# Shift and scale of three column blocks by GpSimd products and ScalarE sums

## The chip, the cores and the metric

The kernel runs on one core of a Trainium2 chip. It is written with the Bass and Tile layers, so the engines of the core (TensorE or PE, VectorE or DVE, ScalarE or ACT, GpSimd or POOL, and SyncE or SP, which here only issues transfers) each run their own list of instructions in order and wait for one another by semaphores. Data lie in the core's SBUF (128 partitions), TensorE writes into PSUM, and transfers between HBM and SBUF are done by 16 DMA engines that take their work from queues.

The metric is the device time of one execution in microseconds; given is the median over several runs. Lower is better.

## The reference

One layer of an adaLN-modulated mixer, D = 2048, 512 latent tokens and 256 context tokens, all in float32. Cut to what matters here:

```python
silu_c = jax.nn.silu(c); silu_cc = jax.nn.silu(c_ctx)
shift, scale, gate       = split(silu_c  @ w_ada + b_ada, 3)     # w_ada: 2048 x 6144
shift_c, scale_c, gate_c = split(silu_cc @ w_ada + b_ada, 3)
h  = rmsnorm(x)   * (1 + scale)   + shift        # 512 x 2048, latent tokens
hc = rmsnorm(ctx) * (1 + scale_c) + shift_c      # 256 x 2048, context tokens
p  = h @ w_in                                    # q, k, v, gates, Fourier input ...
kc, vc = (hc @ w_in)[k and v columns]
y  = merge(attention(q, [k, kc], [v, vc]), fourier_mix(u), gates) @ w_out
out = rmsnorm(x + gate * y)
```

Shift and scale are two vectors of 2048 values for the latent tokens, and two for the context. Each is a product of a row with a 2048 x 2048 matrix. `gate` is needed only at the end, and the context's pair not before the context's rows are made.

## The kernel before, in words

**Precision.** Products of tokens with weights are split: every weight piece `wr` (128x1024, 512 KB) becomes a high part `whi` by a ScalarE copy (L181) and a low part `wlo` by a VectorE subtraction (L182), and TensorE does three products with them (`mm3`, L339 to L341). Most of the kernel is "groups", in which w_in's products are formed by a fast algorithm on such pieces, about 77 us each, and after them the attention with the projections.

**The start stage** (to about 150 us) makes shift and scale, the normalised rows `h` and, as soon as a row block of `h` is there, a first set of products with it (the "start pieces", `w_start`). The 2048 columns are cut into 16 blocks of 128, `kb` = 0 to 15. For block `kb`:

- `wada_load(kb)` brings its weights, two tiles `wa` of 1 MB (pool "wada", four of them, so two blocks at a time), laid out with the input rows on the partitions;
- `modulate(kb)` calls `matvec` (L567) twice: 2 x 16 TensorE instructions of 8 for each half and each k (32 columns of `c2` as the stationary side, of which the first two are silu(c) and silu(c_ctx), 256 weight columns as the moving one: 128 for shift, 128 for scale). In the trace a line of it is `pd<-wa,c`. Both vectors, c and c_ctx, thus cost one pass;
- `taken(kb)` (L583) copies the sums from PSUM to SBUF by ScalarE (tile `ado`); `turned(kb)` (L588) turns them onto the partitions by two TensorE transposes; `factors(kb)` adds the partial sums on VectorE and makes `gain` and `shift`;
- `make_h(kb)` makes the row: VectorE multiplies by gain and by the root (L631), ScalarE adds the shift and rounds to the high part (L632), VectorE makes the low part (L634).

From block 6 on the blocks go in pairs (the loop `for kb in range(4, KK - 4, 2)`, with `k = kb + 2`, so pairs 6/7, 8/9, 10/11, 12/13; 14 and 15 come singly). In a pass of this loop TensorE first works off pieces of the start products with `some(n)`, in between two pieces are split (`split_next`), then come the products of the two blocks, one step of pieces, the four transposes and the two rows.

**What sets the order.** In the start stage PE, ACT and DVE run in the order in which the program writes their instructions (`manual_schedule`). SyncE's loads are chained in the order of `ask` and `load_start`, since each is issued after the last one; a weight tile of the pool must be free before its load is issued. GpSimd's list is the scheduler's; in the start it holds the transfers of the rotary tables: two loads into `S3` and `Z5`, and `rot_d`, which writes the finished tables to DRAM (L767).

**Groups.** Group after group, each in the steps P1, Q5, P2, Q6, P7, Q3, Q4 with four pieces each. Besides, the vector `gate` is made there on VectorE, without TensorE: `use_gate` (L1369) multiplies a piece of `w_gate` (128 output columns on the partitions, 1024 inputs along the row) by silu(c), spread over all partitions in `crow`, and sums along the row. 32 such products are spread by the table GATE_AT over groups 1, 2, 3 and 5, and the rest into the attention. The row is loaded as `c` by GpSimd's queue (`load_row`, first half at the end of group 0, second half at group KV + 1) and made into 2 silu(c) by a ScalarE tanh and one VectorE product (`silu_of_row`); one of the two calls stands in the attention, at step 3.

## Time and profile before

| | |
|---|---|
| median of 3 runs | 1286.51 us (1286.42 to 1286.75) |
| the profiled execution | 1286.97 us |
| its span, first to last instruction | 1285.2 us |
| mean granted clock of TensorE | 0.999 |
| instructions of TensorE, VectorE, ScalarE, GpSimd | 6562, 1305, 1077, 226 |
| VectorE's product and sum for `gate`, each (L1369) | 1217 ns, 32 of them |

The page of the profile gives for each engine the time that it was busy and its share of the span; then the chain of waits, followed back from the last instruction; and groups of equal instructions with their mean time. The timeline lists instructions of one engine in time order: start, length, engine, line, operation, output and inputs, shape, count, and in square brackets how long the engine waited before and for what. The windows give each engine's busy time in stretches of the span. Times are microseconds from the start of the span.

### The profile page before, as it was taken

How to read it: one execution, taken by the hardware profiler on the slowest of the kernel's cores; microseconds unless marked ns; L12 is line 12 of the kernel's file. 1: busy time of each engine (PE TensorE's matmuls, PEld its weight loads, DVE VectorE, ACT ScalarE, POOL GpSimd, SP SyncE). 2: the span in 40 equal slices, each digit the busy share in tenths (PEclk: the TensorE clock that was granted, in tenths of full speed). 3: DMA queues.
4: the chain of work that ended last, by engine and by line, in shares of the span. 5: the costliest groups of instructions: out<-in, count | busy, mean ns of one | idle time of the engine just before them, and what ended most of it. 6: DMA issues, size and time to landing. Idle time of an engine off the chain costs nothing.

```text
span 1285.2 us, 17638 instructions
## 1 busy us (share of the span) xinstructions
PE 1269.6 (99%) x6562; PEld 1045.2 (81%) x6562; DVE 991.0 (77%) x1305; ACT 683.2 (53%) x1077; POOL 173.2 (13%) x226
## 2 busy tenths in 40 slices
PE   8999999999999999999999999999999999999997
PEld 5677888888888888888888888888888888888886
DVE  5767899889778787748687756778898777787677
ACT  5322765555466564543355445766667646465544
POOL 0000121111102011012021011011100221211310
PEclk9999999999999999999999999999999999999999
DMA  9998798888898998887879897578852989998986
GB/s 378 412 368 344 242 204 254 229 240 239 234 315 209 320 271 254 291 197 188 282 204 288 254 259 234 180 234 250 265 178 67 260 241 258 245 207 222 227 207 179
DMA packets 104343, 319.07 MB, mean 248 GB/s; under 512 B 9889, under 2 KB 32801, under 8 KB 100289
## 3 DMA queue, kind: packets, MB, share of 16 engines
q1 hardware_dynamic: 54336, 195.24, 41.8%
q0 software_dynamic: 27600, 100.29, 37.0%
q10 hardware_dynamic: 22320, 22.42, 5.1%
q8 instruction: 51, 0.84, 0.3%
q14 instruction: 36, 0.29, 0.1%
HBM read 283.30 MB, written 34.61 MB: 247 GB/s over the span
## 4 chain that ended last, share of the span: by engine, by line
PE 82%; DVE 3%; DMA 2%; ACT 2%; issue 1%; SPq 0%; ACTq 0%
PE banks L339 10%; PE banks L340 10%; PE banks L341 10%; PE x L341 9%; PE x L339 9%; PE x L340 9%; PE y L341 8%; PE y L340 8%; PE y L339 8%; PE banks L1551 2%; DMA wr<-in_w_pab 1%; DVE wlo L182 1%; DMA s<-yb_d 1%; PE banks L1665 1%; DVE s L182 0%
## 5 line engine op out<-in xcount | busy, mean ns | idle before, releaser
L181 ACT ACTIVATE whi<-R 128x1024 fp32r<-128x1024 f32 x138 | 145.1, 1058 | 143.7 <-PE banks L341 47.5
L182 DVE TENSOR_TENSOR wlo<-R,whi 128x1024 fp32r<-128x1024 f32 x138 | 167.7, 1221 | 61.2 <-ACT whi L181 60.9
L182 DVE TENSOR_TENSOR wlo<-wr,whi 128x1024 fp32r<-128x1024 f32 (+1 forms) x122 | 147.3, 1213 | 62.7 <-ACT whi L181 62.5
L181 ACT ACTIVATE whi<-wr 128x1024 fp32r<-128x1024 f32 (+1 forms) x122 | 127.4, 1050 | 123.4 <-PE y L341 33.0
L339 PE MATMUL banks<-whi,s 128*128 128x512 f32 (+1 forms) x400 | 157.8, 394 | 0.9 <-ACT ev L1160 0.7
L340 PE MATMUL banks<-wlo,s 128*128 128x512 f32 (+1 forms) x400 | 155.9, 390 | 0.0
L341 PE MATMUL banks<-whi,s 128*128 128x512 f32 (+1 forms) x400 | 155.8, 389 | 0.0
L339 PE MATMUL x<-whi,s 128*128 128x512 f32 x352 | 137.1, 390 | 0.0
L341 PE MATMUL x<-whi,s 128*128 128x512 f32 x352 | 137.0, 389 | 0.0
L340 PE MATMUL x<-wlo,s 128*128 128x512 f32 x352 | 136.9, 389 | 0.0
L292 POOL DMA_DIRECT2D R<-in_w_g x68 | 59.5, 874 | 484.7 <-DVE wlo L182 290.2
L340 PE MATMUL y<-wlo,s 128*128 128x512 f32 x316 | 123.0, 389 | 0.1
L339 PE MATMUL y<-whi,s 128*128 128x512 f32 x316 | 122.9, 389 | 0.0
L341 PE MATMUL y<-whi,s 128*128 128x512 f32 x316 | 122.8, 389 | 0.0
L181 ACT ACTIVATE s<-wr 128x512 fp32r<-128x512 f32 (+2 forms) x93 | 60.8, 677 | 66.0 <-DMA wr<-cf_d 24.4
L182 DVE TENSOR_TENSOR s<-wr,s 128x512 fp32r<-128x512 f32 (+2 forms) x93 | 66.7, 749 | 31.8 <-ACT s L181 30.9
L339 PEld LDWEIGHTS banks<-whi,s 128*128 128x128 f32 x400 | 75.2, 188 | 16.6 <-ACT ev L1160 1.1
L341 PEld LDWEIGHTS banks<-whi,s 128*128 128x128 f32 x400 | 75.2, 188 | 15.3
L340 PEld LDWEIGHTS banks<-wlo,s 128*128 128x128 f32 x400 | 75.2, 188 | 13.9 <-DVE wlo L182 0.2
L340 PEld LDWEIGHTS x<-wlo,s 128*128 128x128 f32 x352 | 66.1, 188 | 13.8
L341 PEld LDWEIGHTS x<-whi,s 128*128 128x128 f32 x352 | 66.1, 188 | 13.7
L339 PEld LDWEIGHTS x<-whi,s 128*128 128x128 f32 x352 | 66.1, 188 | 13.6
(333 smaller groups left out, 2794.0 us busy)
## 6 DMA issues: line engine op xcount, KB each, us to landing
wr<-in_w_g SPq DMA_DIRECT2D x124, 512.0 KB, 5.6
R<-in_w_g POOLq DMA_DIRECT2D x68, 512.0 KB, 7.4
wa<-in_w_ss SPq DMA_DIRECT2D x31, 1024.0 KB, 9.5
R<-in_w_g SPq DMA_DIRECT2D x32, 512.0 KB, 5.8
wr<-in_w_gate SPq DMA_DIRECT2D x32, 512.0 KB, 5.1
wr<-in_w_o SPq DMA_DIRECT2D x24, 512.0 KB, 7.1
R<-in_w_o POOLq DMA_DIRECT2D x24, 512.0 KB, 8.9
wr<-in_w_pab SPq DMA_DIRECT2D x20, 512.0 KB, 6.1
```

What stands on the lines that cost most here:

```text
L181: first = nc.scalar.activation(hi, src, ACT.Copy)
L182: return first, nc.vector.tensor_tensor(lo, src, hi.bitcast(F32), op=ALU.subtract)
L292: chained[:] = [nc.gpsimd.dma_start(chain[e.pc], e.nxt, accum_op=ALU.add)]
L339: nc.tensor.matmul(o, ah, bh, start=start, stop=False, skip_group_check=cont)
L340: nc.tensor.matmul(o, ah, bl, start=False, stop=False, skip_group_check=cont)
L341: nc.tensor.matmul(o, al, bh, start=False, stop=stop, skip_group_check=cont)
L1551: nc.tensor.transpose(tp[:, k * P : (k + 1) * P], p[:, k * P : (k + 1) * P], ident)
L1665: last_turn[0] = nc.tensor.transpose(tp[:, k // 2, 256 * (k % 2) + P * t : 256 * (k % 2) + P * t + P], m[:, t, k * P : k * P + P], ident)
```

## The change

Blocks 9, 11 and 13 leave TensorE. For the latent tokens:

- the weights of these three blocks are laid out the other way in HBM: output column on the partition, and for each of shift and scale 2048 inputs along the row. Size and number of their loads stay;
- silu(c) and silu(c_ctx), which VectorE has made at the beginning anyway, are written to DRAM (`c_d`, one GpSimd transfer), and silu(c) comes back spread over the partitions in two loads of 128x1024 (`load_c`, tiles `crw`), 512 KB each in SBUF;
- `weighed(kb)`: GpSimd multiplies the weights by the row in place, four products of 128x1024 a block (L633);
- `summed_up`: ScalarE sums each half block along its row, two instructions of 128x2048 with an accumulated output (L639);
- `of_parts`: two small VectorE instructions make gain and shift from these sums; the reduction of `factors` isn't needed there.

So the pair 8/9 is now: the product of block 8 on TensorE, its copy and its two transposes, while block 9 goes over GpSimd and ScalarE. Pair 10/11 and 12/13 likewise. The loads come in another order, the odd block first: 9, 8, 11, 10, 13, 12, 14, 15.

The context's share of these blocks moves into the groups. Their weights are loaded once more in quarters (twelve pieces of 512 KB), and `use_part` multiplies and sums them on VectorE with silu(c_ctx) in `crow`, six in group 1 and six in group 2 (CTX_AT); `context_factors` makes gain and shift of the context from them in group 3. The six gate products of groups 1 and 2 go to group 4. `load_row` now loads finished silu rows from `c_d`, four times in place of two, and `silu_of_row` is gone. The factor 0.5 of `use_gate` goes with it.

The core of the diff:

```diff
+BY_POOL = (9, 11, 13)
+CTX_PARTS = [(kb, s, h) for h in range(2) for kb in BY_POOL for s in range(2)]
+CTX_AT = {(1 + n // 6, ("Q5", "P2", "Q6", "P7", "Q3", "Q4")[n % 6], 1): n for n in range(len(CTX_PARTS))}
...
-GATE_AT = ([(g, n, 1) for g in (1, 2) for n in ("P2", "Q6", "Q3")] + [(3, "Q5", 1)]
+GATE_AT = ([(3, "Q5", 1), (4, "P1", 1), (4, "Q5", 2)] + [(4, n, 1) for n in ("Q6", "P7", "Q3", "Q4")]
...
+    nc.gpsimd.dma_start(c_d.rearrange("j p k -> p j k"), ce.rearrange("p (j k) -> p j k", j=2))
...
+    def load_c():
+        for h in range(2):
+            c_rows.append(hm.tile([P, 1024], F32, tag=f"s{7 + h}", bufs=1, name=uid("crw")))
+            ask(nc.sync, c_rows[-1], c_half(0, h))
+
+    def weighed(kb):
+        w = [v.rearrange("p k c -> p (k c)") for v in wada.pop(kb)]
+        r = r_of[kb] = pap.tile([P, 2], F32, tag="par", bufs=2, name=uid("par"))
+        for s in range(2):
+            for h in range(2):
+                v = w[s][:, 1024 * h : 1024 * h + 1024]
+                nc.gpsimd.tensor_tensor(v, v, c_rows[h], op=ALU.mult)
+        return w, r
+
+    def summed_up(w, r, line):
+        with behind(line):
+            for s in range(2):
+                nc.scalar.activation(w[s], w[s], ACT.Copy, accum_out=r[:, s : s + 1])
...
                     for k in (6, 7):
                         wada[k] = wada_load(k)
                         load_start()
+                    load_c()
...
             for kb in range(4, KK - 4, 2):
+                k = kb + 2
+                pool = k + 1 in BY_POOL
+                if pool:
+                    parts = weighed(k + 1)
+                    load_next()
                 some(3)
                 split_next()
                 some(5)
                 split_next()
...
-                for i in range(2):
-                    modulate(k + i)
-                    if k + 2 + i < KK:
-                        wada[k + 2 + i] = wada_load(k + 2 + i)
-                        for _ in range(2 if k + 2 + i == KK - 3 else 1):
-                            load_start()
+                if pool:
+                    summed_up(*parts, (last_split[-1][0],))
+                modulate(k)
+                if not pool:
+                    load_next()
+                load_start()
+                if not pool:
+                    modulate(k + 1)
+                load_next()
+                for _ in range(2 if kb == 8 else 1):
+                    load_start()
                 some(1)
-                for i in range(2):
+                for i in range(1 if pool else 2):
                     turned(k + i)
...
+                if pool:
+                    r = r_of.pop(k + 1)
+                    of_parts(k + 1, 0, (r[:, 0:1], r[:, 1:2]))
+                else:
+                    factors(k + 1)
...
+                q = None if self.last else CTX_AT.get((self.g, name, pc))
+                if q is not None:
+                    use_part(get(("ss", q)), cparts2[:, q : q + 1], last_split[-1][1])
```

How the change moves instructions is shown at three places. First SyncE's list where the weights of blocks 8 to 11 are asked for; before, `wa_687` and `wa_689` are the halves of block 8, `wa_712` and `wa_714` of block 9, `wa_824` and `wa_826` of block 10, and `wr` are start pieces. Before:

```order
L217 DMA wr_615<-in_w_start 128x1024
L477 DMA wa_687<-in_w_ss 128x2048
L477 DMA wa_689<-in_w_ss 128x2048
L217 DMA wr_691<-in_w_start 128x1024
L477 DMA wa_712<-in_w_ss 128x2048
L477 DMA wa_714<-in_w_ss 128x2048
L217 DMA wr_716<-in_w_start 128x1024
L477 DMA wa_824<-in_w_ss 128x2048
L477 DMA wa_826<-in_w_ss 128x2048
```

And after, where `wa_695` and `wa_697` are block 9, `wa_720` and `wa_722` block 8, `wa_783` and `wa_785` block 11:

```order
L222 DMA wr_619<-in_w_start 128x1024
L488 DMA crw_621<-c_d 128x1024
L488 DMA crw_623<-c_d 128x1024
L488 DMA wa_695<-in_w_ss 128x2048
L488 DMA wa_697<-in_w_ss 128x2048
L222 DMA wr_699<-in_w_start 128x1024
L488 DMA wa_720<-in_w_ss 128x2048
L488 DMA wa_722<-in_w_ss 128x2048
L222 DMA wr_724<-in_w_start 128x1024
L488 DMA wa_783<-in_w_ss 128x2048
L488 DMA wa_785<-in_w_ss 128x2048
```

The two halves of the spread row stand ahead of block 9, and block 9 ahead of block 8; block 11 follows without a wait for a product of the pair 8/9.

Second, ScalarE's list around the pair 12/13: two splits of pieces (`whi`), the copies of the sums from PSUM (`ado`), and the rounding of row 12 (`s<-xt,shift`). Before, with the copies of blocks 12 and 13:

```order
L632 ACTIVATE s_1015<-xt,shift 128x512 x2
L181 ACTIVATE whi_1068<-wr_853 128x1024
L181 ACTIVATE whi_1087<-wr_997 128x1024
L583 COPY ado_1108<-pd_1091 128x256
L583 COPY ado_1133<-pd_1116 128x256
L632 ACTIVATE s_1157<-xt,shift 128x512 x2
```

After, with the sums of block 13 and the copy of block 12:

```order
L673 ACTIVATE s_993<-xt,shift 128x512 x2
L186 ACTIVATE whi_1053<-wr_849 128x1024
L186 ACTIVATE whi_1072<-wr_977 128x1024
L639 ACTIVATE wa_912,par_1035<-wa_912 128x2048
L639 ACTIVATE wa_914,par_1035<-wa_914 128x2048
L596 COPY ado_1095<-pd_1078 128x256
L673 ACTIVATE s_1119<-xt,shift 128x512 x2
```

The two sums stand between the second split and the copy, and one copy is left.

Third, GpSimd's list after the change, where before only the three transfers of the rotary tables stood (L795, L797 and L808 of the changed kernel):

```order
L795 DMA S_67<-in_rope 128x1024
L797 DMA Z_69<-in_qkg 128x256
L633 TENSOR_TENSOR wa_695<-wa_695,crw_621 128x1024
L633 TENSOR_TENSOR wa_695<-wa_695,crw_623 128x1024
L633 TENSOR_TENSOR wa_697<-wa_697,crw_621 128x1024
L633 TENSOR_TENSOR wa_697<-wa_697,crw_623 128x1024
L808 DMA rot_d<-S_67 128x1024
```

The four products of block 9 come ahead of the transfer of the finished tables to DRAM, and the products of blocks 11 and 13 follow behind it.

More of the change, by code (lines that the diff above doesn't have):

```diff
@@ L123, in block_kernel @@
 @with_exitstack
-def block_kernel(ctx, tc, xT, ctx_rows, ctx_toks, x, c_row, w_ss, w_gate, vecs, qkg, rope, dft_c, dft_s,
+def block_kernel(ctx, tc, xT, ctx_rows, ctx_toks, x, w_ss, w_gate, vecs, qkg, rope, dft_c, dft_s,
                  w_start, w_g, w_pab, w_o, final_g, out):
@@ L436, in block_kernel @@
             for pc in range(4):
-                if (g, name, pc) in GATE_AT:
-                    q = GATE_AT[g, name, pc]
-                    stream(("gate", q), w_gate[q], 1024, 1, "raw")
+                if (g, name, pc) in GATE_AT or (g, name, pc) in CTX_AT:
+                    if (g, name, pc) in GATE_AT:
+                        q = GATE_AT[g, name, pc]
+                        stream(("gate", q), w_gate[q], 1024, 1, "raw")
+                    else:
+                        q = CTX_AT[g, name, pc]
+                        kb, s, h = CTX_PARTS[q]
+                        stream(("ss", q), w_ss[kb].rearrange("p (s h n) c -> s h p (n c)", s=2, h=2)[s, h], 1024, 1, "raw")
                     e = todo.pop()
@@ L1351, in context_row, with load_row, use_part, context_factors @@
         nc.scalar.dma_start(cf_d[i], t)
[L1354 to L1370 removed]
+    crow = [None]
+    def load_row(j, half):
+        crow[0] = rp.tile([P, 1024], F32, tag="raw0", bufs=1, name=uid("crow"))
+        nc.gpsimd.dma_start(crow[0], c_half(j, half))
+    def use_part(w, out, line):
+        with tc.issue_after(line.ins):
+            nc.vector.scalar_tensor_tensor(w, w, 1.0, crow[0], op0=ALU.mult, op1=ALU.mult, accum_out=out)
+    def use_gate(q, w, line):
+        use_part(w, gparts[:, q : q + 1], line)
+    def context_factors():
+        n = len(CTX_PARTS) // 2
+        nc.vector.tensor_tensor(cparts2[:, :n], cparts2[:, :n], cparts2[:, n:], op=ALU.add)
+        for i, kb in enumerate(BY_POOL):
+            of_parts(kb, 1, (cparts2[:, 2 * i : 2 * i + 1], cparts2[:, 2 * i + 1 : 2 * i + 2]))
     qz, qs, kv = {}, {}, {}
@@ L1716, in block_kernel @@
                 give(summed.pop()[0])
-        if i == 3:
-            with tc.issue_after(maxima[0].ins), tc.issue_after(maxima[1].ins):
-                e = take((1024,))
-                silu_of_row(1, e)
-                give(e)
         if i == 33:
```

41 lines of the change are left out of this document (22 added, 19 removed).

## The prediction

> **What bounds the kernel now.** I read the head of the page and the chain of waits first, then the windows, then the timeline of the start stage engine by engine. The profiled execution took 1286.97 us (span 1285.2, and 1.8 around it), 0.46 above the median of 1286.51. The sum below is made against 1286.97 and then lowered by 0.46.
>
> ```profile
> span 1285.2 us, 17638 instructions
> PE 1269.6 (99%) x6562; PEld 1045.2 (81%) x6562; DVE 991.0 (77%) x1305; ACT 683.2 (53%) x1077; POOL 173.2 (13%) x226
> PE 82%; DVE 3%; DMA 2%; ACT 2%; issue 1%; SPq 0%; ACTq 0%
> ```
>
> TensorE has work for 99% of the span and carries 82% of the chain that ended last. So a microsecond less of TensorE is a microsecond gained, if nothing else arrives late. What the change takes from TensorE lies in the start, where weights come in. Columns of the windows: stretch, its length, busy time of PE, PEld, DVE, ACT, POOL, granted clock, DMA share, GB/s.
>
> ```profile
> 20.00:60.00 40.00, 39.10 (x299) 27.31 (x300) 27.51 (x56) 14.50 (x22) 0.30 (x1) 1.00 1.02 414
> 60.00:110.00 50.00, 50.00 (x396) 36.95 (x398) 31.38 (x63) 12.26 (x18) 1.50 (x3) 1.00 0.92 370
> 304.00:381.00 77.00, 77.00 (x341) 63.79 (x340) 60.59 (x76) 42.26 (x82) 10.81 (x12) 1.00 0.87 251
> ```
>
> To 60 us the DMA engines are full, at 414 GB/s; I take that as their limit. From 60 to 110 they fall short of it by a tenth, while TensorE never pauses: the two are nearly level there. In the groups (third row) DMA and VectorE have room. The dips can be seen in slices of 2 us from 50 to 130 us, in the view of the DMA:
>
> ```profile
> GB/s 338 401 422 422 430 426 406 387 408 426 414 422 434 393 123 279 442 418 432 420 434 393 90 369 414 402 438 422 395 55 217 410 416 424 430 414 220 342 170 233
> ```
>
> 78 to 82 us shows 123 and 279, 94 to 98 shows 90 and 369: 795 GB/s short of 414 over 2 us, so 3.84 us of transfer that a fuller queue could take back.
>
> **TensorE, removed.** Two products of a block pair, then the four transposes; further down one block alone:
>
> ```profile
> 62.71 3.66 PE L567 MATMUL pd<-wa,c 128*32 128x256 f32 x64
> ...
> 66.31 0.50 PE L339 MATMUL pc<-s,whi 128*128 128x512 f32 x1
> ...
> 67.80 0.60 PE L588 MATMUL pd<-ident,ado 128*128 128x128 f32 x4
> 68.16 0.48 PE L339 MATMUL pc<-s,whi 128*128 128x512 f32 x1
> ...
> 77.90 3.66 PE L567 MATMUL pd<-wa,c 128*32 128x256 f32 x64
> ...
> 113.32 0.60 PE L588 MATMUL pd<-ident,ado 128*128 128x128 f32 x4
> ...
> 119.34 1.93 PE L567 MATMUL pd<-wa,c 128*32 128x256 f32 x32
> ...
> 121.20 0.50 PE L339 MATMUL pb<-whi,s 128*128 128x512 f32 x1
> ...
> 122.01 0.38 PE L588 MATMUL pd<-ident,ado 128*128 128x128 f32 x2
> 122.14 0.48 PE L339 MATMUL pb<-whi,s 128*128 128x512 f32 x1
> ```
>
> A pair holds TensorE for 66.31 - 62.71 = 3.60 us, one block for 121.20 - 119.34 = 1.86, so a block less saves 1.74. The transposes take 0.36 for two blocks and 0.13 for one: 0.23. That is 1.97 a block and 5.9 us for blocks 9, 11 and 13. This part is certain; the question is what arrives late.
>
> **The spread row's loads.** Two loads of 0.5 MB enter SyncE's queue ahead of block 9's weights: 1.05 MB at 414 GB/s is 2.53 us in which nothing else moves. The view of the DMA has one weight load for each of the windows 63.8 to 64.2 and 67.2 to 67.4 us, the first and the last of the four for blocks 8 and 9 (issued at 63.84 and 67.22); the last column is the time to landing:
>
> ```profile
> wa<-in_w_ss SPq DMA_DIRECT2D x1, 1024.0 KB, 6.3
> wa<-in_w_ss SPq DMA_DIRECT2D x1, 1024.0 KB, 11.7
> ```
>
> Behind 2.53 us more of queue, 70.1 and 78.9 become 72.7 and 81.4. The order is now block 9, then 8. TensorE comes to the product of block 8 at 77.90 and wants its second half 0.9 later, at 78.8; it lands at 81.4. TensorE waits 2.6 us, which is more than block 9 saves. Bounds: 0 if the row came for nothing, 2.6 as the queue stands.
>
> **The GpSimd products.** Twelve, of 128x1024. The trace has none of the kind. One stream of that engine is a memset, 0.53 us for 512 columns, so 1.06 for 1024; a product has three streams, two in and one out: 1.06 to 3.2 us. I take 2.1, two streams, 8.4 a block. [...]
>
> ```profile
> L534 POOL MEMSET s<- 128x512 f32 x1 | 0.5, 530 | 0.0
> L1202 POOL TENSOR_SCALAR small<-small x11: 198/395/1077, 195.7 to 659.7; 128x8 f32<-128x8 f32 x8, 128x4 f32<-128x4 f32 x2, 128x2 f32<-128x2 f32 x1
> 381.79 1.23 DVE L269 TENSOR_TENSOR R<-R,wr 128x1024 f32<-128x1024 f32 x1
> 381.99 1.08 POOL L1202 TENSOR_SCALAR small<-small 128x2 f32<-128x2 f32 x1 [30.91 <-DVE small L1317]
> 661.24 2.32 POOL L1203 TENSOR_TENSOR small<-small,mhalf 128x8 f32<-128x8 f32 x1
> 661.95 1.21 DVE L1221 TENSOR_TENSOR qr<-qr,y 128x1024 f32<-128x1024 f32 x1
> ```
>
> They don't run free. A GpSimd instruction on two columns took 1.08 us where 0.20 is the least, and ended at 383.07, just behind the VectorE sum of two SBUF tiles that ended at 383.02. GpSimd stood still while VectorE read two tiles. In the other direction the last two rows show no delay of VectorE, but that GpSimd instruction reads only 8 columns. [...]
>
> VectorE's own work with two SBUF inputs, as GpSimd meets it with block 9:
>
> ```profile
> 73.48 0.75 DVE L634 SCALAR_TENSOR_TENSOR s<-xt,shift,s 128x512 fp32r<-128x512 f32 x1 [0.19 <-ACT s L632]
> 74.75 2.35 DVE L182 TENSOR_TENSOR wlo<-wr,whi 128x1024 fp32r<-128x1024 f32 x2
> 77.02 1.28 DVE L761 SCALAR_TENSOR_TENSOR S<-S,Z 128x512 f32<-128x512 f32 x2
> ```
>
> 4.4 us. The products begin at 72.7 and, taking turns, end at 72.7 + 8.4 + 4.4 = 85.5. The DMA of the turned tables stands behind them in GpSimd's queue; its readers come later than 86 and I cost it at nothing.
>
> **The ScalarE sums.** ScalarE takes 0.62 us for 512 columns and 1.05 for 1024, so 1.05 + 2 x 0.43 = 1.91 for 2048, 1.95 with the accumulator's write: two a block, 3.9.
>
> ```profile
> L181 ACT ACTIVATE whi<-wr 128x1024 fp32r<-128x1024 f32 x16 | 16.5, 1050 | 11.1 <-DMA wr<-in_w_start 11.1
> L181 ACT ACTIVATE s<-wr 128x512 fp32r<-128x512 f32 x4 | 2.4, 622 | 1.5 <-DMA wr<-in_w_g 1.5
> 110.40 1.06 ACT L181 ACTIVATE whi<-wr 128x1024 fp32r<-128x1024 f32 x1 [5.72 <-DMA wr<-in_w_start]
> 111.36 0.35 ACT L583 COPY ado<-pd 128x256 f32<-128x256 f32 x1
> ```
>
> They stand in ScalarE's order in front of the copy that TensorE's transposes of the even block wait for. With block 9: the second sum begins at 85.5 and ends at 87.4, the copy at 87.8. TensorE has finished block 8 at 82.3 and six matmuls (66.31 to 67.80) at 83.8, and waits 4.0. Block 9 in all: 2.6 + 4.0 - 1.97 = **+4.6**.
>
> With block 13 the same copy also stands behind the split for which ScalarE waited 5.72 us before, until its load landed at 110.40. That load is the last of a full queue: 110.40 + 2.53 - 3.84 = 109.1 at the earliest. Split 1.06, sums 3.9, copy 0.36: 114.4, where the transposes began at 113.32 before. Less 0.23, this stretch can't end earlier than **+0.9** whatever GpSimd costs, so all 5.9 us saved are gone by 114 us.
>
> **Blocks 11 and 13 beside VectorE.** Their weights land while VectorE makes rows 8 to 11, which TensorE takes next:
>
> ```profile
> 70.75 0.75 DVE L634 SCALAR_TENSOR_TENSOR s<-xt,shift,s 128x512 fp32r<-128x512 f32 x1 [0.23 <-ACT s L632]
> 72.37 0.39 PE L339 MATMUL pb<-whi,s 128*128 128x512 f32 x1
> ```
>
> Such a row was ready at 71.50 and first read by the third matmul from 72.37, at 72.8: 1.3 us in hand. One product of 2.1 in front of it costs 0.8, two cost 2.9, and late sums could cost 4.0 as above. I take 1.8 for block 11 and 2.9 for block 13: with 1.97 saved each, -0.2 and +0.9. Bounds -2.0 and +2.0 each, as far as the floor of +0.9 lets them.
>
> **Groups and attention.** VectorE gets twelve context products in groups 1 and 2, where it had six gate products (the seventh stays), which move to group 4, and loses two of 1.22 us; by the row each is 1.22:
>
> ```profile
> L1369 DVE SCALAR_TENSOR_TENSOR wr<-wr,crow x32: 1204/1217/1220, 256.8 to 982.3; 128x1024 f32<-128x1024 f32 x32
> ```
>
> Three more a group against 16.4 us idle of 77 (row 304 to 381): hidden, 0. Their loads, 1.5 MB a group at 251 of 414 GB/s, too. Without that cover: 6 x 1.22 = 7.3. In the attention ScalarE and VectorE lose one instruction each and the scheduler sets a few rows otherwise: 0, up to 1 either way.
>
> **Sum.** +4.6 - 0.2 + 0.9 = +5.3, so 1292.3 beside the profiled execution and 1291.8 as a median. At products of 3.2, block 9 costs 4.4 more; without anything held up, only +0.9 stays.
>
> **The rivals.**
> - *GpSimd is quick enough or undisturbed*: products of 1.06 that VectorE holds up end at 72.7 + 4.2 + 4.4 = 81.3, and products of 2.1 that nothing holds up at 81.1; either way the sums are done before 85.1 and the copy comes near 83.8. The start then ends by the load queue, at +0.9: 1287.4, no change. For it: the second pair of rows above. Against: the first.
> - *TensorE sets the pace all through* (the other side): the decisive point is the copy of block 12, ready by 107.4 instead of 114.4 (113.32 less 5.9). It needs the row's 2.53 us to vanish in the dips, and sums that fit into ScalarE's 5.72 us of waiting ahead of that split rather than behind it. All of it gives -5.9: 1280.6; the row alone for nothing gives -1.6: 1284.9. Against: the order of ScalarE and the full queue.
> - *The groups run late*: VectorE or the raw tiles don't carry twice as many pieces; up to +7.3 on top, 1294 to 1299. Against: nine such pieces stand in group 5 already.
>
> **How the numbers follow.** My forecast, held-up products, 0.55; undisturbed 0.28; TensorE pacing 0.12; late groups 0.05. About 0.2% (2.6 us) is what a measurement of this kernel can tell from no change. Faster 0.12, same 0.28, slower 0.60. The range goes down to the row that costs nothing (1284.9), which takes in the undisturbed case with 1 us for the attention and about half of the pacing one. Above, it takes blocks 11 and 13 at their upper bounds (+4.6 + 2.0 + 2.0, less 0.46: 1294.7) and half of what products of 3.2 add to block 9 (2.2): 1296.9. The slower cases alone lie from 1289.2, where the measurement begins to tell, to 1296.9.
>
> **What would show it.** Right: PE waits for `w_ss` at the product of block 8 by some 2.6 us; PE waits for the ado copies of blocks 8 and 12; GpSimd products of unequal length, the long ones ending just behind a VectorE sum of two SBUF tiles; block 13's ScalarE sums behind the last split and the transposes of block 12 at 116 us or later; the same distance between before and after from 150 us to the end. Wrong: products all of one length near 1 us, no new idle time of TensorE before 115 us, the transposes of block 12 before 111, or a difference that arises only in the groups or the attention.

## The result, and the profile after

The changed kernel takes 1314.49 us (median of 6 runs, 1313.44 to 1316.26) where the kernel before took 1286.63 beside it. The ratio is 1.0216, with a 95% interval from 1.0203 to 1.0229: 27.9 us slower. The forecast was 1291.8, with a range up to 1296.9. The sign was right; the size was short by 22.7 us.

The head of the page after, with the engines' busy times and the chain of waits by engine:

```profile
span 1312.8 us, 17512 instructions
PE 1275.4 (97%) x6460; PEld 1045.5 (80%) x6460; DVE 1023.7 (78%) x1331; ACT 688.2 (52%) x1083; POOL 209.3 (16%) x241
PE 79%; DMA 8%; DVE 8%; issue 2%; ACT 2%; POOL 1%; SPq 0%; DVEq 0%; ACTq 0%; POOLq 0%
```

TensorE has 102 matmul instructions less in the records and is busy 5.8 us longer. Its share of the chain fell from 82 to 79%; DMA rose from 2 to 8% and VectorE from 3 to 8%. So it waits more, and some of its own time has grown.

Where that is, a comparison of TensorE's matmuls shows: both kernels do the same ones in the same order, apart from the products of `modulate` and the transposes. For the last such matmul before a given time I take its start in both traces and subtract. The steps between the points are how much was lost in each stretch:

| stretch (time in the kernel before) | start, 70 to 150 | groups 0 and 1 | group 2 | group 3 | group 4 | 536 us to the end | sum at the end |
|---|---|---|---|---|---|---|---|
| changed kernel | +13.3 | +0.1 | +5.6 | 0 | +10.4 | -2.2 | +27.5 |

(0.3 us arose before 70 us.) Two places: the start, where I had forecast 5.3, and groups 2 and 4, where I had forecast nothing. The windows of the start after; the columns are as in the prediction, the last three granted clock, DMA share and GB/s:

```profile
70.00:80.00 10.00, 8.94 (x45) 6.75 (x47) 9.54 (x12) 4.83 (x5) 6.61 (x3) 1.00 1.01 425
80.00:90.00 10.00, 7.34 (x49) 4.41 (x39) 8.82 (x6) 2.90 (x5) 8.54 (x5) 0.83 0.67 213
90.00:100.00 10.00, 5.72 (x23) 3.77 (x22) 9.62 (x10) 1.77 (x3) 7.16 (x3) 1.00 1.00 419
100.00:110.00 10.00, 9.95 (x67) 6.99 (x67) 8.13 (x17) 6.34 (x8) 1.42 (x1) 1.00 0.56 205
110.00:120.00 10.00, 5.66 (x19) 3.55 (x18) 9.81 (x9) 2.97 (x4) 8.87 (x4) 0.81 0.75 307
```

Wherever GpSimd is busy (8.54, 7.16, 8.87 of 10 us), VectorE is "busy" too, at 8.8 to 9.8 of 10, with fewer instructions than before, and TensorE stands still for up to 4.3 of 10 us. And the clock falls to 0.83 and 0.81, where it was 1.00 in these stretches before. The two engines side by side, first two lines of VectorE's timeline of row 8 in the kernel before:

```profile
83.99 0.29 DVE L600 TENSOR_SCALAR gain<-adr,bsc,small 128x2 f32<-128x2 f32 x1
85.86 0.75 DVE L634 SCALAR_TENSOR_TENSOR s<-xt,shift,s 128x512 fp32r<-128x512 f32 x1 [0.16 <-ACT s L632]
```

And after the change, of the rows 8 and 9:

```profile
88.32 3.70 DVE L613 TENSOR_SCALAR gain<-adr,bsc,small 128x2 f32<-128x2 f32 x1
91.92 0.22 DVE L615 TENSOR_SCALAR shift<-adr,small 128x2 f32<-128x2 f32 x1
...
93.59 2.40 DVE L675 SCALAR_TENSOR_TENSOR s<-xt,shift,s 128x512 fp32r<-128x512 f32 x1 [0.19 <-ACT s L673]
...
96.10 2.16 DVE L644 TENSOR_TENSOR shift<-par,small 128x1 f32<-128x1 f32 x1
```

Then GpSimd's timeline at that time, and the group of its products:

```profile
87.26 4.72 POOL L633 TENSOR_TENSOR wa<-wa,crw 128x1024 f32<-128x1024 f32 x2
93.06 5.18 POOL L633 TENSOR_TENSOR wa<-wa,crw 128x1024 f32<-128x1024 f32 x2 [1.08 <-DMA wa<-in_w_ss]
```

```profile
L633 POOL TENSOR_TENSOR wa<-wa,crw 128x1024 f32<-128x1024 f32 x12 | 32.0, 2695 | 23.8 <-DMA wa<-in_w_ss 23.7
```

A gain of two columns, 0.29 us before, takes 3.70 and ends at 92.02, just behind two products (2.40 and 2.37 us, one behind the other) that end at 91.98. A shift of one column takes 2.16 and ends with the product at 98.25. In this view a wait of VectorE for GpSimd isn't idle time: it stands in the duration of the instruction that waits, without a bracket, as the 3.70 us show. (The expectations below speak of a port; that is only the author's name for these waits, and what lies behind them no trace shows.) The shortest products take 2.4 us (4.72 for two); the mean of 2.70 has longer ones in it, up to 3.35 us beside a split on VectorE.

What came of it at TensorE, in its timeline of the start (only rows with idle time ahead of them):

```profile
76.40 0.50 PE L346 MATMUL pb<-whi,s 128*128 128x512 f32 x1 [0.41 <-DVE s L675]
79.61 1.07 PE L580 MATMUL pd<-wa,c 128*32 128x256 f32 x16 [0.65 <-DMA wa<-in_w_ss]
82.00 1.93 PE L580 MATMUL pd<-wa,c 128*32 128x256 f32 x16 [1.32 <-DMA wa<-in_w_ss]
87.56 0.44 PE L601 MATMUL pd<-ident,ado 128*128 128x128 f32 x2 [1.34 <-ACT ado L596]
93.46 0.50 PE L344 MATMUL pc<-s,whi 128*128 128x512 f32 x1 [2.72 <-DVE part L701]
96.05 0.50 PE L346 MATMUL pb<-whi,s 128*128 128x512 f32 x1 [0.48 <-DVE s L675]
99.73 0.50 PE L344 MATMUL pb<-whi,s 128*128 128x512 f32 x1 [1.08 <-ACT s L673]
...
111.59 0.50 PE L346 MATMUL pb<-whi,s 128*128 128x512 f32 x1 [0.28 <-DVE s L675]
117.45 0.79 PE L344 MATMUL pb<-whi,s 128*128 128x512 f32 x1 [3.25 <-ACT s L673]
119.47 0.79 PE L346 MATMUL pb<-whi,s 128*128 128x512 f32 x1 [0.80 <-DVE s L675]
```

0.4 us at row 7, 2.0 for the load of block 8, 1.3 for the sums ahead of the copy, and 8.6 for rows 8 to 11 (4.3 for each pair), which VectorE and, behind it, ScalarE delivered late: 12.3.

The loads go later too. Block 11 doesn't wait for TensorE, but it takes the tiles of block 9: its halves go out at 80.67 and 87.28 us, right behind ScalarE's two sums of that block, and block 10 behind them at 88.20, where the kernel before asked for it at 79.03. Between the halves SyncE asks for nothing, and the DMA share from 80 to 90 us is 0.67. TensorE waited for no load between 84 and 163 us, so no cost of it shows here.

### The profile page after: what moved, and what is told of

It reads as the page before. It is cut to its first block, busy times and chain, and to the rows that moved or that the text cites. A ratio compares the mean times of both kernels' runs of the same rounds, so it can differ in the third digit from the quotient of the medians.

```text
span 1312.8 us, 17512 instructions
## 1 busy us (share of the span) xinstructions
PE 1275.4 (97%) x6460; PEld 1045.5 (80%) x6460; DVE 1023.7 (78%) x1331; ACT 688.2 (52%) x1083; POOL 209.3 (16%) x241
## 4 chain that ended last, share of the span: by engine, by line
PE 79%; DMA 8%; DVE 8%; issue 2%; ACT 2%; POOL 1%; SPq 0%; DVEq 0%; ACTq 0%; POOLq 0%
PE banks L344 11%; PE banks L345 10%; PE banks L346 10%; PE x L345 7%; PE x L346 7%; PE x L344 7%; PE y L345 6%; PE y L346 6%; PE y L344 6%; DMA wr<-in_w_g 4%; PE banks L1617 2%; DVE wlo L187 2%; DMA wa<-in_w_ss 2%; PE pd L580 1%; DMA wr<-cf_d 1%
## 5 line engine op out<-in xcount | busy, mean ns | idle before, releaser
L187 DVE TENSOR_TENSOR wlo<-wr,whi 128x1024 fp32r<-128x1024 f32 (+1 forms) x123 | 152.3, 1243 | 71.5 <-ACT whi L186 71.3
L344 PE MATMUL y<-whi,s 128*128 128x512 f32 x320 | 125.1, 391 | 3.7 <-ACT whi L186 3.7
L346 PE MATMUL y<-whi,s 128*128 128x512 f32 x320 | 124.9, 391 | 0.0
```

The source lines that it names most:

```text
L187: return first, nc.vector.tensor_tensor(lo, src, hi.bitcast(F32), op=ALU.subtract)
L344: nc.tensor.matmul(o, ah, bh, start=start, stop=False, skip_group_check=cont)
L346: nc.tensor.matmul(o, al, bh, start=False, stop=stop, skip_group_check=cont)
```

## The experiments

Each table row is read like the one above: us lost by TensorE in each stretch against the trace before.

| run | time | start | groups 0, 1 | group 2 | group 3 | group 4 | 536 us to the end |
|---|---|---|---|---|---|---|---|
| start_alone | 1299.27 | +12.6 | -0.6 | 0 | 0 | 0 | -0.3 |
| groups_alone | 1302.17 | -0.1 | +1.0 | +3.3 | +0.8 | +10.4 | -1.3 |
| no_products | 1306.61 | +4.1 | -0.1 | +6.8 | 0 | +9.7 | -2.0 |
| vector_products | 1305.87 | +2.1 | +0.3 | +4.1 | +3.7 | +9.8 | -2.2 |
| vector_no_row | 1304.44 | +2.8 | +0.1 | +4.5 | +0.2 | +11.6 | -2.0 |
| one_input | 1308.99 | +8.9 | -0.6 | +5.6 | 0 | +11.2 | -2.1 |
| idle_products | 1304.73 | 0 (+20.2 before 70 us) | -0.1 | 0 | 0 | 0 | -1.7 |
| idle_at_pairs | 1298.17 | +10.8 | 0 | 0 | 0 | 0 | -1.2 |
| short_sums | 1300.48 | 0 | +0.4 | +4.1 | +3.4 | +6.2 | -0.9 |
| no_pieces | 1285.66 | 0 | -0.6 | 0 | 0 | 0 | -1.6 |
| not_at_p7 | 1293.75 | 0 | +0.4 | +0.3 | +1.9 | +4.7 | -1.7 |
| three_a_group | 1298.93 | 0 | +0.5 | 0 | +3.1 | +9.3 | -1.7 |
| one_buffer_less | 1291.66 | 0 | +0.2 | +1.6 | +2.9 | +2.1 | -1.2 |
| row_from_dram | 1285.34 | 0 | +0.1 | 0 | 0 | 0 | -1.5 |

(What arose before 70 us, 0.2 to 0.6, is left out. The kernel before took 1285.8 to 1286.8 beside these runs.)

### One cause or two

`start_alone`: the change to the start, with groups and attention as before.

```diff
-CTX_AT = {(1 + n // 6, ...[n % 6], 1): n for n in range(len(CTX_PARTS))}
+    nc.gpsimd.memset(gain, 0.0)
+    nc.gpsimd.memset(shift, 0.0)
```

> Blocks 9, 11 and 13 as in the changed kernel, but groups, gate products and attention as before; the context's share of these blocks is left out (zero). In the changed kernel TensorE was 13.7 us late at 150 us, 5.6 more in group 2, 10.4 more in group 4, and had 2 back at the end. Theory: start and groups are two causes that add up; here only the start's 13.7 stays: 1300, within 1.5. Rival: the late start shifts the loads of the groups against each other and the stalls in groups 2 and 4 follow from it: then 1314 here too.

`groups_alone`: the start before, groups and attention as changed.

```diff
-            next_loads = [9, 8, 11, 10, 13, 12, 14, 15]
-                    parts = weighed(k + 1)
...
+                for i in range(2):
+                    modulate(k + i)
```

> The start as before; the groups and the attention as changed (six context products in groups 1 and 2 each, six gate products in group 4). The weights of the context products are read from the old layout, so the context's share is not the reference's. Theory of two causes: +5.6 in group 2, +10.4 in group 4, -2 after it: 1300.6. Rival (the groups stall only because the start was late): 1285, at most 1287.

1299.27 and 1302.17: 13.0 and 15.9 over the kernel before, 28.9 together where the whole change costs 27.9. Two causes that add up: behind the start as before the changed groups still stall, and behind the changed start the groups as before don't. The rival with one cause is gone.

### The start: who holds whom

`no_products`: the row is loaded and ScalarE sums, but GpSimd does nothing.

```diff
-                nc.gpsimd.tensor_tensor(v, v, c_rows[h], op=ALU.mult)
```

> The changed kernel without the twelve GpSimd products; the row is loaded, ScalarE sums the raw weights. Theory: VectorE stood still behind GpSimd's products (its instructions with SBUF inputs took up to 3.7 us in place of 0.3) and that made the start late; without them the start is at most 3 us late (the row's loads at block 8, the sums in front of the copy): 1300 to 1304 with the groups' 14. Rival: the row's loads and ScalarE's sums made it: the start stays 8 us late or more, 1309 and up.

The start loses 4.1 in place of 13.3, so 9.2 us go with the products; the total, 1306.61, is 2.6 above the upper end that I had expected, for the remaining start was 4.1 and not 3. What remains, in TensorE's timeline of this run:

```profile
79.84 1.07 PE L580 MATMUL pd<-wa,c 128*32 128x256 f32 x16 [1.58 <-DMA wa<-in_w_ss]
82.23 1.93 PE L580 MATMUL pd<-wa,c 128*32 128x256 f32 x16 [1.32 <-DMA wa<-in_w_ss]
116.53 0.69 PE L601 MATMUL pd<-ident,ado 128*128 128x128 f32 x2 [3.40 <-ACT ado L596]
```

That is the row's price at block 8 (2.9 against 2.6 forecast) and block 13's sums ahead of the copy of block 12 (3.4). Both were in the prediction. ScalarE no longer waits for products here, so the 9.2 are not VectorE's waits alone; `idle_at_pairs` below shows these by themselves.

`vector_products`: product and sum in one VectorE instruction, four a block, ahead of the second split.

```diff
-                nc.gpsimd.tensor_tensor(v, v, c_rows[h], op=ALU.mult)
-                nc.scalar.activation(w[s], w[s], ACT.Copy, accum_out=r[:, s : s + 1])
+                nc.vector.scalar_tensor_tensor(v, v, 1.0, c_rows[h], op0=ALU.mult, op1=ALU.mult,
+                                               accum_out=r[:, 2 * h + s : 2 * h + s + 1])
```

> Product and sum of the three blocks in one instruction of VectorE each (128x1024, four a block, 4.9 us) ahead of the second split, in place of GpSimd's products and ScalarE's sums. VectorE was idle for 4.9, 4.5 and 3.6 us before the rows of these pairs. [...] Rival (VectorE has no room for it, whoever else reads): 3 x 4.9 us less the 5.9 saved, start 9 late: 1309.

```profile
L636 DVE SCALAR_TENSOR_TENSOR wa<-wa,crw 128x1024 f32<-128x1024 f32 x12 | 14.0, 1220 | 0.0
```

VectorE does in 1.22 us what GpSimd does in 2.4 and ScalarE sums in another 0.95 (1.90 for 2048 columns), and the start loses only 2.1. VectorE, which was to be kept free of the products, had room for them. I had expected the start between 2 early and 3 late, and 1299 to 1304 in all. (The total, 1305.87, was 2 above that end: group 3 cost 3.7 here and 0 in the changed kernel.)

`one_input`: GpSimd scales by 0.5 in place of the product.

```diff
-                nc.gpsimd.tensor_tensor(v, v, c_rows[h], op=ALU.mult)
+                nc.gpsimd.tensor_scalar(v, v, 0.5, None, op0=ALU.mult)
```

> The changed kernel with GpSimd's products replaced by a scaling by 0.5, which reads one SBUF tile in place of two (weights x 0.5 are summed, so shift and scale of the three blocks are left out). Theory that every GpSimd instruction of this length holds VectorE for its duration: if one takes about 1.1 to 1.6 us, the start is some 8 to 10 late, total 1308 to 1311. [...]

```profile
L633 POOL TENSOR_SCALAR wa<-wa 128x1024 f32<-128x1024 f32 x12 | 34.6, 2906 | 20.1 <-DMA wa<-in_w_ss 20.1
```

The expectation doesn't hold as stated, and neither does its opposite, a VectorE that isn't held at all and a total of 1306. The total of 1308.99 lies in the expected range, but for another reason: the scaling isn't 1.1 to 1.6 us long, two take 5.52 (from 86.02 us) and the mean is 2.91, longer than the product's 2.70. VectorE is taken up less beside it: from 80 to 90 us it is busy for 3.81 us while GpSimd is for 9.42, where the changed kernel has 8.82 and 8.54. TensorE's waits here are 5.6 us for copies behind the sums (1.5 and 4.1), 2.9 for loads and 0.6 for VectorE: the 8.9 come mainly from GpSimd's own length ahead of the sums, and hardly from VectorE being held.

`idle_products`: the kernel before with twelve products that nothing reads.

```diff
+                    with tc.issue_after(last_split[-1][1].ins):
+                        for _ in range(4):
+                            nc.gpsimd.tensor_tensor(idle[0], idle[0], idle[1], op=ALU.mult)
```

> The kernel before, unchanged but for twelve GpSimd products of 128x1024 on constants that nothing reads, four behind the first split of each of the pairs 8/9, 10/11, 12/13. No load, sum or order differs. Theory of the port: VectorE's instructions with SBUF inputs wait for GpSimd, the rows come late and TensorE, which has 1.3 us in hand, waits: 3 to 9 us slower, 1289 to 1295. Rival, that in the changed kernel VectorE's rows were late because of loads and order: no change, within 0.5.

It came out 18.8 us slower, at another place than meant: nothing made the products wait for data, and they ran in one row from 17.5 us on, where the first rows are made. GpSimd's timeline and then VectorE's:

```profile
17.48 31.68 POOL L853 TENSOR_TENSOR idle<-idle,idle 128x1024 f32<-128x1024 f32 x12
```

```profile
22.67 2.10 DVE L600 TENSOR_SCALAR gain<-adr,bsc,small 128x2 f32<-128x2 f32 x1
24.68 0.22 DVE L602 TENSOR_SCALAR shift<-adr,small 128x2 f32<-128x2 f32 x1
24.81 2.66 DVE L621 TENSOR_SCALAR xt<-S,gain 128x512 f32<-128x512 f32 x1
27.57 2.65 DVE L625 SCALAR_TENSOR_TENSOR s<-xt,shift,s 128x512 fp32r<-128x512 f32 x1
30.14 3.11 DVE L182 TENSOR_TENSOR wlo<-wr,whi 128x768 fp32r<-128x768 f32 x1
```

Before, the same five took 0.29, 0.22, 0.48, 0.75 and 0.96 us. GpSimd's work has no reader, no load, no sum; it holds VectorE all the same. `idle_at_pairs` then tied the products to the rows, so that they start near where the changed kernel's do (73.2, 90.8 and 110.6 us against 73.4, 87.3 and 108.6; the diff leaves out how the shapes are rearranged):

```diff
+                if kb >= 6:
+                    for _ in range(4):
+                        nc.gpsimd.tensor_tensor(idle[0], xt[:, kb : kb + 2, :], idle[1], op=ALU.mult)
```

> The kernel before with twelve GpSimd products of 128x1024 that nothing reads, now each four tied to the rows just made (they read rows 6 and 7, 8 and 9, 10 and 11), so that they start where the changed kernel's did in the undisturbed order, near 73, 88 and 103 us. Loads, sums, order of the other engines as before. Theory of the port: VectorE waits up to 2.4 us at each instruction with SBUF inputs that meets a product, but it has 4 to 5 us idle ahead of each pair of rows: 1 to 5 us slower, 1287 to 1291. Rival, that VectorE's held rows alone make the start's 9 us between the runs with and without products: 1295.

1298.17: here the rival's number is the nearer one. TensorE loses 10.8 us in the start, though nothing else is changed; 1.7 of it is a stretch of half clock (last section). VectorE's timeline while row 9 and two rows of tables are made:

```profile
91.49 2.30 DVE L634 SCALAR_TENSOR_TENSOR s<-xt,shift,s 128x512 fp32r<-128x512 f32 x1 [0.19 <-ACT s L632]
93.72 2.34 DVE L642 TENSOR_TENSOR d<-shift 128x1 f32<-128x1 f32 x1
95.98 0.41 DVE L643 TENSOR_TENSOR S<-xt 128x256 f32<-128x256 f32 x1
96.32 2.59 DVE L644 SCALAR_TENSOR_TENSOR Z<-xt,d 128x256 f32<-128x256 f32 x1
98.83 2.32 DVE L642 TENSOR_TENSOR d<-shift 128x1 f32<-128x1 f32 x1
```

Four instructions of 0.75, 0.15, 0.48 and 0.15 us take 9.55 instead of 1.53: here the wait goes by how many of VectorE's instructions meet a product, not by their size. GpSimd's four products beside them run from 90.84 to 101.13 us, 2.57 each, and the last of the four instructions ends at 101.15. The subtraction among them took 0.41, as before. The 4 to 5 us of idle time that VectorE has ahead of each pair were no cover, because the short instructions stand in a row behind it.

`vector_no_row`: as vector_products, with numbers from another tile in place of the loaded row.

```diff
-                    load_c()
+                        c_rows.append(xt[:, 2 * h : 2 * h + 2, :].rearrange("p a c -> p (a c)"))
```

> As the run with products on VectorE, but the spread row isn't loaded; the products take other numbers that lie in SBUF, so the three blocks come out as other values. In that run TensorE waited 3.3 us at block 8, and the start was 2.5 late. Theory (the row's 2.5 us in a full queue make it): the start comes out 0 to 1 us early; with the groups' 16 1302.5 to 1304. Rival (the load of block 8 is late for another reason, the order 9 before 8): 1305.5 as before.

At block 8 the wait is gone, so the row had made it. But the start isn't better (2.8 against 2.1, where 0 to 1 us early was expected): TensorE now waits 3.6 us behind block 10, for VectorE. Taking the row away uncovers the next bound, and I found no version of the start that keeps any of the 5.9 us.

### The groups: time, transfer or buffer

The eighteen added or moved pieces occupy VectorE, the transfers, and the five buffers for raw pieces. `short_sums` cuts the first, `no_pieces` the other two.

```diff
-            nc.vector.scalar_tensor_tensor(w, w, 1.0, crow[0], ...
+            nc.vector.scalar_tensor_tensor(w[:, :n], w[:, :n], 1.0, crow[0][:, :n], ...      # n = 16
```

> The groups alone (start as before), but in groups 1, 2 and 4 the products with the spread row take 16 of 1024 columns: the rest of context and gate is left out. The pieces are loaded as before and held until then. Theory that the buffers of raw pieces set it (SyncE's loads wait for one, then VectorE for 7 us for a load): the time stays near 1302, at least 1297. Rival, VectorE's 1.22 us each: 1287, at most 1290.

```diff
-                    use_part(get(("ss", q)), cparts2[:, q : q + 1], last_split[-1][1])
+                    use_part(crow[0], cparts2[:, q : q + 1], last_split[-1][1])
```

> The groups alone again, now with all 18 products of groups 1, 2 and 4 at full size, but on the row itself: their pieces aren't loaded, so context and gate miss these parts. Theory of the buffers: the stalls of groups 2 and 4 go, 1286 to 1288. Rival, VectorE's time: stays near 1302.

With VectorE's time taken away 1300.48 remain; with the pieces taken away the time is that of before (ratio 1.0000, 0.9989 to 1.0012), with all products at full size. The windows of groups 2 and 4 of `no_pieces`:

```profile
304.00:381.00 77.00, 77.00 (x342) 63.75 (x341) 67.71 (x86) 45.05 (x84) 13.30 (x15) 1.00 0.87 253
458.00:535.00 77.00, 77.00 (x341) 63.81 (x340) 62.66 (x90) 39.03 (x51) 7.03 (x8) 1.00 0.90 276
```

VectorE has 67.7 of 77 us (60.6 before), and TensorE doesn't pause. So the step of the prediction that hid VectorE's time was right by itself; it is the pieces that cost. Once they stall the groups, VectorE's time has a say too: `short_sums` loses 6.2 in place of 10.4 in group 4, but 3.4 in place of 0.8 in group 3. How they do it shows in group 4 of `groups_alone`, in the timelines of SyncE's queue, of VectorE and of TensorE:

```profile
497.04 0.33 SPq L222 DMA_DIRECT2D wr<-in_w_gate  x1
504.76 13.24 SPq L222 DMA_DIRECT2D wr<-in_w_g  x4
```

```profile
515.21 1.23 DVE L282 TENSOR_TENSOR wr<-R,wr 128x1024 f32<-128x1024 f32 x1 [7.00 <-DMA wr<-in_w_g]
```

```profile
517.09 0.80 PE L345 MATMUL x<-s,s 128*128 128x512 f32 x1 [3.32 <-DVE s L187]
```

SyncE issues in order and asks for nothing between 497.4 and 504.8, since the buffer for its next piece comes free only at 504.74, when VectorE has split an earlier one; then four loads go out over 13 us, VectorE stands for 7.0 waiting for one, and TensorE for 3.3.

`not_at_p7` and `three_a_group` moved the pieces:

```diff
-... (4, "Q5", 2)] + [(4, n, 1) for n in ("Q6", "P7", "Q3", "Q4")]      ("Q5", "P2", "Q6", "P7", "Q3", "Q4")[n % 6]
+... (4, "Q5", 2)] + [(4, n, 1) for n in ("P2", "Q6", "Q3", "Q4")]      ("P1", "Q5", "P2", "Q6", "Q3", "Q4")[n % 6]
```

> The groups alone (start as before), all eighteen pieces loaded and used, but none at step P7: in groups 1 and 2 at P1, Q5, P2, Q6, Q3, Q4, in group 4 at P1, Q5, P2, Q6, Q3, Q4. The stalls of groups 2 and 4 lay where the pieces of P7 come; of the steps only P2, P7 and Q3 take raw buffers for their own pieces. Theory that the piece at P7 is the one too many: the stalls shrink to a third or less, 1285 to 1291. Rival, six in a group are too many wherever they are: 1298 to 1303. The context's share of three blocks is not the reference's.

```diff
-CTX_AT = {(1 + n // 6, ("Q5", "P2", "Q6", "P7", "Q3", "Q4")[n % 6], 1): n for n in range(len(CTX_PARTS))}
+CTX_AT = {(1 + n // 6, ("P2", "Q6", "Q3")[n % 6], 1): n for n in (0, 1, 2, 6, 7, 8)}
...
+ (3, "P2", 1), (3, "Q6", 1), (3, "Q3", 1)] + [(4, n, 1) for n in ("P2", "Q6", "Q3")]
```

> The groups alone with three pieces in groups 1, 2 and 4, at P2, Q6 and Q3, as the kernel before had them, and four in group 3; six of the twelve context products are left out. Theory of the buffers: no stall in groups 1, 2 and 4, 1285 to 1287. Rival (any extra loads beside the context's rows stall): 1290 and up.

`not_at_p7` came out between theory and rival; `three_a_group`, at 1298.93, lies where its rival put it. Three pieces a group cost nothing in groups 1 and 2, as before; in groups 3 (four pieces) and 4 (three) they cost 3.1 and 9.3, the latter nearly what six did. There the context's rows come as raw pieces too, so a place that is free in one group isn't in the next. Without a piece at P7 half of the stalls go (7.6 lost up to 536 us in place of 16.0). Place matters and number matters; one simple rule of mine for either was wrong.

`one_buffer_less` takes a buffer from the kernel before and adds no load:

```diff
+            elif (g, name) == (1, "P1"):
+                raw_pools.remove((rp, 1, "raw1", 1))
             elif (g, name) == (KV - 1, "Q3"):
-                raw_pools.remove((rp, 1, "raw1", 1))
```

> The kernel before with four in place of five buffers for raw pieces from group 1 on (the fifth was given up at the end of group 4 anyway); no piece, load or product is added. Theory that an added piece costs because it holds a buffer: TensorE stalls in groups 1 to 4 as with the added pieces, 3 us or more slower, 1289 and up. Rival, the added 512 KB loads themselves are what is late: no change.

1291.66 over four runs from 1288.9 to 1294.2 (ratio 1.0032, 1.0005 to 1.0060): stalls in groups 2, 3 and 4 with no transfer added. A held buffer alone can do it: 6.6 us in the three groups of the traced run. Whether it is all of the 10.4 in group 4 stays open: one buffer less costs 2.1 there, and the DMA engines are full in that stretch, so the added transfers may have their part. Two windows of `groups_alone`, then two of the kernel before:

```profile
490.00:500.00 10.00, 10.00 (x45) 8.26 (x45) 8.99 (x18) 6.72 (x11) 0.00 (x0) 1.00 1.01 352
...
505.00:515.00 10.00, 8.77 (x39) 6.94 (x37) 3.21 (x5) 1.15 (x2) 0.88 (x1) 1.00 1.02 245
```

```profile
500.00:505.00 5.00, 5.00 (x24) 4.14 (x23) 3.80 (x5) 2.12 (x2) 0.86 (x1) 1.00 1.03 283
505.00:515.00 10.00, 10.00 (x45) 8.28 (x45) 4.60 (x5) 2.21 (x3) 0.00 (x0) 1.00 1.05 279
```

The share of 1.01 and 1.02 says that the engines were never free there, with SyncE's loads held or not. But they are as full before (1.03 and 1.05) without a stall, and the loads are no slower: SyncE's loads of 499.0, 500.2 and 508.3 us landed 10.4 to 13.5 us later before, those of 504.8 to 507.1 in `groups_alone` 10.4 to 13.0. This speaks for loads that are asked for late, and not for slower transfers; that the added transfers delay the release of a buffer further up isn't excluded.

### The part that gains

In all runs with the changed groups TensorE makes up 1 to 2 us behind 536 us against the trace before. `row_from_dram` is the kernel before with silu(c) from DRAM in place of `silu_of_row`:

```diff
-                silu_of_row(1, e)
...
+                load_row(*row_at)
```

> The kernel before with one thing of the change alone: silu(c) goes to DRAM early and comes back spread, so that tanh and product in group 1 and in the attention go. All 18 runs of the groups so far gained 1 to 1.5 us in the attention against the 0.5 that the early transfer cost in the start. Theory: the gain is this edit's: 0.5 to 1.5 us faster. Rival, it comes from the order of rows or the gate pieces moved: no change.

TensorE gains 1.5 us there and loses 0.5 before 70 us. The time is 1285.34 against 1285.9, ratio 0.9992 (0.9983 to 1.0001): the direction of the theory, but not told from no change. And the 1.5 us aren't shown to be this edit's: `idle_products`, `idle_at_pairs` and `one_buffer_less`, which touch neither the row nor anything behind 536 us, make up 1.7, 1.2 and 1.2 there against the same trace. A wait of 0.8 us at 846 us in that trace is missing in all of these and in `row_from_dram`, so much of the gain lies in that one trace. No run was clearly faster than the kernel before.

## Why the prediction was wrong

- **TensorE, removed (5.9 us): right as a price, but nothing of it was left.** Over the products of the pairs 10/11 and 12/13 TensorE's lag against the trace before falls by 1.95 us each, 1.97 forecast. `vector_products`, which removes the same, still loses 2.1.
- **The row's loads (2.6 at block 8): right.** 2.9 in `no_products`; gone in `vector_no_row`.
- **The length of a product (2.1): nearly right**, 2.4 measured. Block 9's products were to end at 85.5 and ended at 85.2, which is partly luck: they began 0.7 later and were longer than assumed, and GpSimd waited some 2.2 us for VectorE (11.82 for the four against 4 x 2.4) in place of 4.4.
- **VectorE and GpSimd waiting for each other: right in kind, and the step that failed in the start.** The prediction let GpSimd wait for VectorE's long sums (4.4 us) and priced the other direction at "one product of 2.1 in front of it costs 0.8, two cost 2.9", once for each of blocks 11 and 13 (4.7 together) and not at all for block 9. No row of the kernel before shows VectorE waiting for a product: that price was the author's estimate, and no run shows it; the runs show the waits that follow. It should have counted VectorE's instructions that meet a product, and for each the rest of that product: for rows 8 and 9 the waits of 3.4, 1.65 and 2.0 us, for rows 10 and 11 1.5, 2.0, 2.2 and 1.2, each taken as the duration over that of before. TensorE stood 8.6 us for it at these rows and 0.4 at row 7. `idle_at_pairs` shows that products alone, with no load or sum changed, cost 10.8 us with what they bring along. The floor of +0.9 by the load queue never came to bear.
- **The sums ahead of the copy: right in kind.** The two sums of a block, estimated at 3.9, took 3.78 (block 11, 101.48 to 105.26 us). Forecast 4.0 at block 8 and measured 1.3, since TensorE itself came later; 3.4 at block 12 in `no_products`.
- **The clock: not in the prediction.** TensorE at half clock is a cost that its waits brought with them, 4.1 us in the start (last section).
- **The groups (0): the step that failed by most.** VectorE's time was hidden, as predicted, but I took the loads for hidden "at 251 of 414 GB/s". The changed groups cost 15.5 us in `groups_alone` (1.0, 3.3, 0.8 and 10.4) and nothing in `no_pieces`. The row that this was read from gives a DMA share of 0.87 beside the 251 GB/s, by which the engines had 13% of their time left and not 39%; and no term asked when a buffer is free. The rival "groups run late" named the raw tiles but was priced by VectorE's time (at most 7.3) and given 0.05. That a held buffer alone stalls the groups is shown (6.6 in `one_buffer_less`); how the 15.5 divide between buffers and transfers stays open. The sign "the same distance between before and after from 150 us to the end" failed by this.
- **The range.** Its upper end takes the 0.46 off twice: by its own terms 1286.51 + 4.6 + 2.0 + 2.0 is 1295.1, and the end 1297.3. The measured time lies outside of that too.

In the start, 12.3 us of idle rows and 4.1 of half clock less the 5.9 saved make 10.5 of the 13.3. Shorter gaps give only 0.2 (TensorE is idle for 12.5 us in all from 70 us to the end of the start, and in the kernel before for none). The remaining 2.6 lie in its busy time: at six of the waits its lag grows by 0.16 or 0.17 us more than the wait itself (0.57 for the 0.41 at row 7), and the ten waits together would give some 1.6, an estimate; for the rest no cause is known. In the prediction's terms: the row and the copy cost 3.3 in place of 6.6, the rows 9.0 in place of 4.7, and 6.9 came with the waits that had no term.

## What to carry to other kernels

Work given to GpSimd did not run beside VectorE's work here: count VectorE's instructions on SBUF data that fall into its span, and price each at up to a whole product, however short it is itself (here waits of 1.2 to 2.2 us beside products of 2.4 to 2.8, and once 3.4); a chain of short ones on the critical path was the worst neighbour (1.53 us became 9.55 in `idle_at_pairs`). Before work is moved to a helper, look whether the engine that it is to spare could do it in its idle time. And before calling a load hidden, read the DMA engines' share of busy time and not only the GB/s (0.87 stood beside 251 of 414 here), and count the buffers that are free at that step.

## What the runs showed that was not expected

**Half clock after a half-idle stretch.** Windows of the changed kernel, cut where the granted clock changes:

```profile
78.60:82.00 3.40, 1.43 (x18) 0.50 (x17) 3.40 (x2) 2.00 (x2) 3.40 (x3) 1.00 1.04 361
82.00:85.40 3.40, 3.40 (x20) 1.84 (x21) 3.40 (x2) 0.15 (x1) 3.21 (x1) 0.50 0.74 287
112.80:116.20 3.40, 1.40 (x7) 0.79 (x5) 3.40 (x2) 0.00 (x0) 3.40 (x3) 0.99 0.99 409
116.20:119.60 3.40, 1.35 (x3) 0.63 (x3) 3.21 (x5) 2.57 (x3) 2.67 (x1) 0.50 0.37 148
119.60:123.00 3.40, 3.40 (x8) 2.67 (x9) 3.40 (x8) 3.40 (x4) 0.00 (x0) 0.51 0.02 5
372.00:375.50 3.50, 0.54 (x4) 0.12 (x2) 3.50 (x5) 1.64 (x3) 0.00 (x0) 1.00 0.98 194
375.50:378.90 3.40, 3.40 (x8) 2.73 (x9) 3.40 (x5) 1.01 (x2) 0.00 (x0) 0.51 0.87 228
```

Half clock runs from 81.99 to 85.41, from 116.13 to 122.95, from 375.54 to 378.95 and from 546.21 to 549.62 us, once or twice 3.41 us, and the distances from each start to the next are 10, 76 and 50 times that. In the rows above each stretch behind one in which TensorE was busy for 1.43 us or less runs at half clock; 1.43 of 3.40 us, busy for 42%, was enough. (It isn't a strict threshold: from 3.5 to 6.9 us of the same run it was busy for 1.33, with full clock behind it.) From 90 to 100 us, where it was busy 5.72 of 10, the clock stayed full. In the start three stretches with 8.15 us of work cost 4.1 that way, half of them, and a stall in the groups that brings one such stretch costs up to 1.7 more; both are estimates.

**Short instructions that waited, and some that didn't.** Among VectorE's instructions that waited are scalings of a single SBUF tile by a value for each partition (gain, 128x2, 3.70 us, 0.29 before). The same scaling of one column (0.26 us at 95.92 and 111.46 in the changed kernel) went on within the span of a product, and so did those that read PSUM (`part<-pc,part`, 0.68 us at 76.27 and 116.56) and the small reductions from PSUM (0.17 us at 88.11). Beside GpSimd's one-input scaling VectorE was taken up less (3.81 us from 80 to 90, above); no run shows why.
